# SSD scan: sample states on row quarters of TensorE, the D x term on VectorE, a held mask piece and later transposes of y

## The chip, the cores and the metric

One core of a Trainium2 chip runs the whole step. The metric is the device time of one execution in microseconds; the profile is one execution taken by the hardware profiler. Engines are named as in the profile: PE is TensorE, PEld its weight loads, DVE VectorE, ACT ScalarE, POOL GpSimd, SP SyncE.

## What is computed

One step of a hybrid encoder: a Mamba-2 (SSD) mixer, a PEER mixer, attention with a window, and a second PEER mixer, over 256 frames of one new stream and 16 frames of each of 8 running streams (384 rows in three blocks of 128; the third block holds the 8 samples, 16 rows each). The change lies in the SSD mixer, which in the reference comes to this:

```python
xbc, conv_new = causal_conv(xbc, conv_prev, conv_w, conv_b)      # 4 taps, then silu
dt = softplus(dt_raw + dt_bias); A = -exp(a_log)
acum = cumsum(dt * A)                                            # inside a chunk of 64 frames
lmat = exp(where(causal, acum_i - acum_j, -inf))
y_diag = einsum('bcijgr,bcjgrp->bcigrp', cb[..., None] * lmat, x * dt)      # cb = C B^T
states = einsum('bcjgn,bcjgrp->bcgrpn', B, x * dt * exp(acum_end - acum))
s_fin, s_prev = scan(s * chunk_decay + states)
y = y_diag + einsum('bcign,bcgrpn->bcigrp', C, s_prev) * exp(acum)
y = rmsnorm((y + x * d_skip) * silu(z)) @ w_out
```

There are 32 heads of 64 channels in 8 groups, a state of 128 for each, and for the 8 running streams an old state per head that is decayed, updated and written out.

## The kernel before

The scan runs over the eight groups, `for g in range(GROUPS)`. For each group four convolution tiles are made: `b_tile`, `c_tile`, `x_tile(0)`, `x_tile(1)`. One is a gemm of 24 matmuls of 128x384 (L130 to L132, high and low halves of an fp32 split) into one PSUM bank, copies by ScalarE, a first tap by ScalarE (L368), three taps by VectorE (L371), and a silu by ScalarE (L373, L374). The split of each block of weights is a cast by ScalarE (L105, `hi`) and a subtraction by VectorE (L106, `lo`). `gate` is the gemm for z (L425 to L427).

`decay` builds the masked decay matrix `ab`: twelve VectorE pieces (L438), one exponential by ScalarE (L441, before which it loads a table, as it does again for the next silu), the product C B^T on TensorE (L444) and one VectorE product (L446); it also transposes B (L449) and copies it (L451) and, with ScalarE, makes eight copies of the sample block of B, each masked to one sample (L453). `tokens` transposes x (L461) and scales it (L463). A group later, `states` makes the prompt's states (L471 to L475); `outputs` sums per head the D x term (a diagonal `dg`, made by POOL at L397, times `xs`, L483) and the masked product (L487) in PSUM, makes the old-state term (L490, and L494 on column quarters of the array), and VectorE puts y together (L499 to L503). `turn` transposes y (L512) and splits it (L108, L109) for w_out. `carry` decays the samples' old states (L518), computes the eight samples' new states as eight matmuls over all 128 rows with the masked copies (L523) into four banks, and adds them (L525).

After the eight groups the product with w_out runs over 16 blocks of channels (`out_terms`); the last group's states and outputs come at block 2, its turn at 5, its carry at 7. Six PSUM banks are its accumulators; there are eight in all.

A scheduler sets the order of each engine's instructions from its own estimate of times; each engine runs its list strictly in that order. `pin` is the one means by which the program forces a place: the instruction stays behind the one that the program wrote just before it for the same engine.

## Time and profile before

| | us |
|---|---|
| median of 3 runs | 2582.8 |
| lowest and highest | 2578.8, 2591.1 |
| the profiled execution | 2576.94 |
| its span | 2575.2 |
| PE busy in the span | 2425.7 |
| DVE busy | 1927.6 |
| ACT busy | 1313.5 |
| POOL busy | 683.2 |

The share of busy time is a mean over stages with different limits. The scan and w_out fill the first 400 us, the first peer layer follows, then attention and the second peer layer. A stage is read by its own stretch, and an order by the timeline. A row that has no bracket at its end followed the row before it on its engine without a wait.

### The profile page before, as it was taken

The numbers are of one execution on the slowest core, as the hardware profiler recorded it, in microseconds if no ns is written. First come the engines' busy times: TensorE is split into PE (matmuls) and PEld (weight loads), VectorE is DVE, ScalarE is ACT, GpSimd is POOL, SyncE is SP. The second block draws the span as 40 slices with busy tenths as digits, with TensorE's granted clock in tenths as the row PEclk, the third lists the DMA queues.
The fourth block names the chain that finished last, engine by engine and source line by source line (L and its number), as shares of the span: only waits on it lengthen the run. The fifth ranks groups of instructions, "written<-read, shape, count | busy, mean of one in ns | idle before, by whom it ended". The sixth has DMA issues, their size and how long they took to land. (4 is left out here: it accounts for less than half of the span.)

```text
span 2575.2 us, 45047 instructions
## 1 busy us (share of the span) xinstructions
PE 2425.7 (94%) x16816; PEld 2055.6 (80%) x16816; DVE 1927.6 (75%) x4206; ACT 1313.5 (51%) x2522; POOL 683.2 (27%) x749
## 2 busy tenths in 40 slices
PE   8999999999899999999998998999899999999998
PEld 7999988988789976666666878998789976667666
DVE  5877746989989988765455656989989988765445
ACT  5756524433456666554444544443456665554444
POOL 2222200033332244432331100033332244433331
PEclk9999999999999999999999989999999999999999
DMA  5545434478888899988886314478788898888886
GB/s 183 181 168 178 147 128 148 146 263 276 266 297 285 296 323 334 350 306 307 318 319 208 125 42 157 140 270 274 263 294 286 294 333 330 339 302 305 302 315 231
DMA packets 179117, 645.62 MB, mean 251 GB/s; under 512 B 24193, under 2 KB 26097, under 8 KB 176241
## 3 DMA queue, kind: packets, MB, share of 16 engines
q1 hardware_dynamic: 99632, 366.90, 40.6%
q0 software_dynamic: 79264, 275.84, 31.1%
q8 instruction: 132, 2.16, 0.3%
q14 instruction: 89, 0.72, 0.1%
HBM read 626.43 MB, written 18.06 MB: 250 GB/s over the span
## 5 line engine op out<-in xcount | busy, mean ns | idle before, releaser
L105 ACT CAST hi<-raw 128x1024 fp32r<-128x1024 f32 (+1 forms) x616 | 641.5, 1042 | 650.5 <-PE bank L131 425.7
L106 DVE TENSOR_TENSOR lo<-raw,hi 128x1024 fp32r<-128x1024 f32 (+1 forms) x616 | 750.0, 1218 | 234.3 <-ACT hi L105 233.2
L1072 POOL DMA_INDIRECT gath<-in_p_u,eidU x256 | 297.8, 1163 | 796.6 <-DVE gath L1109 424.0
L132 PE MATMUL bank<-xhi,lo 128*128 128x256 f32 (+1 forms) x1344 | 408.3, 304 | 12.6 <-DVE lo L106 12.5
L130 PE MATMUL bank<-xhi,hi 128*128 128x256 f32 (+1 forms) x1344 | 404.2, 301 | 4.2 <-ACT hi L105 4.2
L131 PE MATMUL bank<-xlo,hi 128*128 128x256 f32 (+1 forms) x1344 | 398.5, 297 | 0.0
L132 PE MATMUL bank<-qhi,lo 128*128 128x256 f32 (+1 forms) x1152 | 349.0, 305 | 29.7 <-DVE lo L106 29.5
L130 PE MATMUL bank<-qhi,hi 128*128 128x256 f32 (+1 forms) x1152 | 348.3, 303 | 19.6 <-ACT hi L105 12.0
L1109 DVE SCALAR_TENSOR_TENSOR gath<-gath,xg 128x1024 f32<-128x1024 f32 x256 | 311.8, 1218 | 50.2 <-DMA gath<-in_p_u,eidU 50.1
L131 PE MATMUL bank<-qlo,hi 128*128 128x256 f32 (+1 forms) x1152 | 344.3, 299 | 0.0
L143 PE MATMUL bank<-lo,phi 128*128 128x512 f32 x1024 | 331.6, 405 | 6.3 <-DVE lo L106 5.9
L143 PE MATMUL bank<-hi,plo 128*128 128x512 f32 x1024 | 322.7, 397 | 0.0
L143 PE MATMUL bank<-hi,phi 128*128 128x512 f32 x1024 | 291.6, 405 | 16.8 <-ACT hi L105 13.6
L105 ACT CAST phi<-G 128x256 fp32r<-128x256 f32 x256 | 103.4, 405 | 378.7 <-PE bank L143 264.9
L1072 POOL DMA_INDIRECT gv<-in_p_v,eidT x180 | 203.6, 1131 | 326.0 <-PE bank L1126 277.2
L132 PEld LDWEIGHTS bank<-xhi,lo 128*128 128x128 f32 x1344 | 255.4, 190 | 20.0 <-DVE lo L106 17.6
L143 PEld LDWEIGHTS bank<-hi,phi 128*128 128x128 f32 x1024 | 186.3, 189 | 96.4 <-ACT hi L105 41.0
L130 PEld LDWEIGHTS bank<-xhi,hi 128*128 128x128 f32 x1344 | 255.9, 190 | 8.8 <-ACT hi L105 5.2
L131 PEld LDWEIGHTS bank<-xlo,hi 128*128 128x128 f32 x1344 | 255.6, 190 | 0.3
L132 PEld LDWEIGHTS bank<-qhi,lo 128*128 128x128 f32 x1152 | 223.3, 195 | 36.5 <-DVE lo L106 36.2
L130 PEld LDWEIGHTS bank<-qhi,hi 128*128 128x128 f32 x1152 | 223.7, 194 | 23.5 <-ACT hi L105 15.1
L143 PEld LDWEIGHTS bank<-lo,phi 128*128 128x128 f32 x1024 | 187.2, 190 | 66.5 <-DVE lo L106 16.5
(343 smaller groups left out, 3889.1 us busy)
## 6 DMA issues: line engine op xcount, KB each, us to landing
raw<-in_u_t SPq DMA_DIRECT2D x256, 512.0 KB, 4.6
raw<-in_p_v SPq DMA_DIRECT2D x256, 512.0 KB, 5.5
raw<-in_w_in SPq DMA_DIRECT2D x32, 512.0 KB, 4.8
raw<-in_p_w_q SPq DMA_DIRECT2D x32, 512.0 KB, 5.5
s<-in_state_ssm SPq DMA_DIRECT2D x8, 1024.0 KB, 4.8
raw<-in_w_z SPq DMA_DIRECT2D x16, 512.0 KB, 3.8
out_sm_ssm<-s SPq DMA_DIRECT2D x8, 1024.0 KB, 4.2
raw<-in_w_out SPq DMA_DIRECT2D x16, 512.0 KB, 4.3
```

The source lines that it names most:

```text
L105: act.copy(hi, raw)
L106: dve.tensor_tensor(lo, raw, hi32, op=OP.subtract)
L130: pe.matmul(ps, whi[:, s], xhi[:, k, c0:c1], start=(k == 0), stop=False)
L131: pe.matmul(ps, whi[:, s], xlo[:, k, c0:c1], start=False, stop=False)
L132: pe.matmul(ps, wlo[:, s], xhi[:, k, c0:c1], start=False, stop=(k == KD - 1))
L143: mm = pe.matmul(ps, x, w[:, hf * n:(hf + 1) * n], start=s_, stop=e_)
L1072: pool.indirect_dma_start(out=tile_, out_offset=None, in_=tab, in_offset=bass.IndirectOffsetOnAxis(ap=idx, axis=0))
L1109: pin(dve.scalar_tensor_tensor(tile_, tile_, 1.0, xg[g], op0=OP.mult, op1=OP.mult, accum_out=au[g][:, j:j + 1]))
```

## The change

It does four things. The samples' states are made by eight matmuls that each read 32 of the 128 rows (two samples) with a mask that keeps one of the two, so `Bt` has two masked copies in place of eight; quarter q writes bank q, and both passes `w` go round the four banks; each is pinned. The D x term leaves TensorE: VectorE computes x times `dsk` into y where it scales x, the old-state term goes to a tile `yo` of its own, and y is summed from the three; the factor silu(z) is applied to the whole of y at the end. In `decay` the first of the twelve mask pieces is pinned behind the VectorE instruction written just before, which is the last tap of the convolution before it (of `x_tile(1)` of the same group, and for group 0 of `c_tile` of group 1); the decay of the old states is pinned behind `turn`. The transposes of y and the carry are called between `x_tile(0)` and `x_tile(1)`, and not before `x_tile(0)` (for group 0, after `x_tile(1)` of group 1).

```diff
@@ -253,8 +253,7 @@
-            dsk = T(one, [P, 16], F32, tag="dsk")
-            sync.dma_start(dsk, t_in["d_skip"])
+            dsk = brow(t_in["d_skip"], HEADS, one, "dsk")
 
...
+            parm = T(one, [P, 2], F32, tag="parm")
...
                     dve.tensor_scalar(seqm, iob[:, :NSEQ], seqf, None, op0=OP.is_equal)
+                    dve.tensor_reduce(parm, seqm.rearrange("p (q w) -> p w q", w=2), axis=AX.X, op=OP.add)
@@ -392,9 +394,6 @@
...
                         self.s0 = T(two, [P, NSEQ, 256], F32, tag="s0")
                         sync.dma_start(self.s0, t_in["state_ssm"][g])
-                        self.dg = T(two, [P, 2, P], F32, tag="dg", bufs=1)
-                        for j in range(2):
-                            pool.tensor_scalar(self.dg[:, j], ident, dsk[:, 2 * g + j:2 * g + j + 1], None, op0=OP.mult)
 
                     def b_tile(self):
                         self.BT = T(two, [P, NT], F32, tag="BT")
@@ -435,9 +434,9 @@
                         ab = self.ab
                         for rr in range(4):
                             for b in range(NB):
-                                dve.scalar_tensor_tensor(ab[:, rr, b], ab[:, rr, b],
+                                (pin if rr + b == 0 else lambda i_: i_)(dve.scalar_tensor_tensor(ab[:, rr, b], ab[:, rr, b],
                                                          acum[:, b, 4 * g + rr:4 * g + rr + 1], msk[:, b],
-                                                         op0=OP.subtract, op1=OP.add)
+                                                         op0=OP.subtract, op1=OP.add))
                         act.activation(ab, ab, AF.Exp)
                         cb = bank([P, NB, P])
                         for b in range(NB):
@@ -447,14 +446,15 @@
                         pb = bank([P, NB, P])
                         for b in range(NB):
                             pe.transpose(pb[:, b], BT[:, b * P:(b + 1) * P], ident)
-                        self.Bt = Bt = T(two, [P, 2 + NSEQ, P], F32, tag="Bt", bufs=1)
+                        self.Bt = Bt = T(two, [P, 4, P], F32, tag="Bt", bufs=1)
                         act.copy(Bt[:, 0:2], pb[:, 0:2])
-                        for i in range(NSEQ):
-                            act.activation(Bt[:, 2 + i], pb[:, 2], AF.Copy, scale=seqm[:, i:i + 1])
+                        for w in range(2):
+                            act.activation(Bt[:, 2 + w], pb[:, 2], AF.Copy, scale=parm[:, w:w + 1])
 
                     def tokens(self):
                         self.xdt = T(two, [P, NB, 256], F32, tag="xdt", bufs=1)
                         self.xde = T(two, [P, NB, 256], F32, tag="xde", bufs=1)
+                        self.y = T(two, [P, NB, 256], F32, tag="y", bufs=1)
                         for b in range(NB):
                             px = bank([P, 256])
                             for j in range(2):
@@ -462,6 +462,8 @@
                             for o, sc in ((self.xdt, dt), (self.xde, ddt)):
                                 dve.tensor_tensor(heads(o[:, b]), heads(px),
                                                   sc[:, b, self.hs].unsqueeze(2).to_broadcast([P, 4, 64]), op=OP.mult)
+                            dve.tensor_tensor(heads(self.y[:, b]), heads(px),
+                                              dsk[:, self.hs].unsqueeze(2).to_broadcast([P, 4, 64]), op=OP.mult)
 
                     def states(self):
 
@@ -479,13 +481,9 @@
                         pY = [bank([P, 256]), bank([P, 2, 256])]
                         for b in range(NB):
                             o = pY[0] if b == 0 else pY[1][:, b - 1]
-                            for j in range(2):
-                                pe.matmul(o[:, j * P:(j + 1) * P], self.xs[:, j, b * P:(b + 1) * P], self.dg[:, j],
-                                          start=True, stop=False)
-                                for rr in (2 * j, 2 * j + 1):
-                                    cs = slice(64 * rr, 64 * rr + 64)
-                                    pe.matmul(o[:, cs], self.ab[:, rr, b], self.xdt[:, b, cs], start=False,
-                                              stop=(rr == 2 * j + 1))
+                            for rr in range(4):
+                                cs = slice(64 * rr, 64 * rr + 64)
+                                pe.matmul(o[:, cs], self.ab[:, rr, b], self.xdt[:, b, cs], start=True, stop=True)
                         pO = bank([P, 2, 256])
                         pe.matmul(pO[:, 0], self.CT[:, P:2 * P], self.st[:, 0], start=True, stop=True)
                         for w in range(2):
@@ -494,13 +492,15 @@
                                 pe.matmul(pO[rows, 1], self.CM[:, w, q].rearrange("p w t -> p (w t)"),
                                           self.s0[:, 2 * q + w], start=(w == 0), stop=(w == 1),
                                           tile_position=(0, 32 * q))
-                        y = self.y = T(two, [P, NB, 256], F32, tag="y", bufs=1)
-                        y12 = y[:, 1:].rearrange("p b (r d) -> p b r d", d=64)
-                        dve.tensor_tensor(y12, pO.rearrange("p b (r d) -> p b r d", d=64),
+                        y = self.y
+                        yo = T(two, [P, 2, 256], F32, tag="yo", bufs=1)
+                        dve.tensor_tensor(yo.rearrange("p b (r d) -> p b r d", d=64),
+                                          pO.rearrange("p b (r d) -> p b r d", d=64),
                                           etok[:, :, self.hs].unsqueeze(3).to_broadcast([P, 2, 4, 64]), op=OP.mult)
-                        dve.tensor_tensor(y[:, 0], self.zs[:, 0], pY[0], op=OP.mult)
+                        dve.tensor_tensor(y[:, 1:], y[:, 1:], yo, op=OP.add)
+                        dve.tensor_tensor(y[:, 0], y[:, 0], pY[0], op=OP.add)
                         dve.tensor_tensor(y[:, 1:], y[:, 1:], pY[1], op=OP.add)
-                        dve.tensor_tensor(y[:, 1:], y[:, 1:], self.zs[:, 1:], op=OP.mult)
+                        dve.tensor_tensor(y, y, self.zs, op=OP.mult)
                         for b in range(NB):
                             act.activation(self.zs[:, b], y[:, b], AF.Square, accum_out=ssq[:, b, g:g + 1])
 
@@ -515,12 +515,16 @@
                     def carry(self):
 
                         s0 = self.s0
-                        dve.tensor_tensor(s0.rearrange("p s (r d) -> p s r d", d=64),
-                                          s0.rearrange("p s (r d) -> p s r d", d=64),
-                                          decS[:, :, self.hs].unsqueeze(3).to_broadcast([P, NSEQ, 4, 64]), op=OP.mult)
+                        pin(dve.tensor_tensor(s0.rearrange("p s (r d) -> p s r d", d=64),
+                                              s0.rearrange("p s (r d) -> p s r d", d=64),
+                                              decS[:, :, self.hs].unsqueeze(3).to_broadcast([P, NSEQ, 4, 64]),
+                                              op=OP.mult))
                         pss = [bank([P, 2, 256]) for _ in range(4)]
-                        for i in range(NSEQ):
-                            pe.matmul(pss[i // 2][:, i % 2], self.Bt[:, 2 + i], self.xde[:, 2], start=True, stop=True)
+                        for w in range(2):
+                            for q in range(4):
+                                rows = slice(32 * q, 32 * q + 32)
+                                pin(pe.matmul(pss[q][:, w], self.Bt[rows, 2 + w], self.xde[rows, 2],
+                                              start=True, stop=True, tile_position=(32 * q, 0)))
                         for k in range(4):
                             dve.tensor_tensor(s0[:, 2 * k:2 * k + 2], s0[:, 2 * k:2 * k + 2], pss[k], op=OP.add)
 
@@ -548,16 +552,17 @@
                     if g == 0:
                         st_ = steps()
                         next(st_)
-                    if g > 1:
-                        prev.turn()
                     G_.x_tile(0)
                     if g == 1:
                         prev.states()
                         prev.outputs()
+                    elif g:
                         prev.turn()
-                    if g:
                         prev.carry()
                     G_.x_tile(1)
+                    if g == 1:
+                        prev.turn()
+                        prev.carry()
                     if g == 0:
                         G_.gate()
                         next(st_, None)
@@ -1323,7 +1328,7 @@
     a["conv_b"] = f["m_conv_b"][0].reshape(32, P).T
     a["dt_bias"] = f["m_dt_bias"][0]
     a["a_log"] = f["m_a_log"][0]
-    a["d_skip"] = np.repeat(f["m_d_skip"][0], 64).reshape(16, P).T
+    a["d_skip"] = f["m_d_skip"][0]
     a["m_norm"] = f["m_norm"][0].reshape(16, P).T
     a["w_out"] = f["m_w_out"][0]
     a["state_conv"] = f["state_conv"][0].reshape(NSEQ, 3, 32, P).transpose(3, 2, 0, 1)
```

What this does to the order on the engines at three places:

TensorE in a steady group, before: states (L471), outputs (L483 to L494), and further down the samples' states (L523) with the transposes of y (L512).

```order
L471 MATMUL bank_1945<-xde_1875,Bt_1771 128x256
L483 MATMUL bank_1951<-dg_1533,xs_1641 128x128
L471 MATMUL bank_1945<-xde_1875,Bt_1771 128x256
L487 MATMUL bank_1951<-xdt_1874,ab_1529 128x64 x2
L483 MATMUL bank_1951<-dg_1533,xs_1641 128x128
L487 MATMUL bank_1951<-xdt_1874,ab_1529 128x64 x2
L483 MATMUL bank_1952<-dg_1533,xs_1641 128x128
L487 MATMUL bank_1952<-xdt_1874,ab_1529 128x64 x2
```

```order
L523 MATMUL bank_2096<-xde_1875,Bt_1771 128x256 x2
L523 MATMUL bank_2097<-xde_1875,Bt_1771 128x256 x2
L523 MATMUL bank_2098<-xde_1875,Bt_1771 128x256 x2
L523 MATMUL bank_2099<-xde_1875,Bt_1771 128x256 x2
L512 MATMUL bank_2037<-ident_69,y_1981 128x128 x2
L512 MATMUL bank_2043<-ident_69,y_1981 128x128 x2
```

The same places after the change (line numbers differ: L473 is L471, L486 is L487, L488 is L490, L492 is L494, L526 is L523):

```order
L473 MATMUL bank_2307<-xde_2236,Bt_2138 128x256
L486 MATMUL bank_2313<-xdt_2235,ab_1904 128x64 x3
L473 MATMUL bank_2307<-xde_2236,Bt_2138 128x256
L486 MATMUL bank_2313<-xdt_2235,ab_1904 128x64
L486 MATMUL bank_2314<-xdt_2235,ab_1904 128x64 x8
L488 MATMUL bank_2327<-st_2306,CT_1948 128x256
L492 MATMUL bank_2327<-s_314_1906,cm_55_247 32x256 x8
```

```order
L512 MATMUL bank_2440<-ident_69,y_2237 128x128 x3
L512 MATMUL bank_2446<-ident_69,y_2237 128x128 x3
L526 MATMUL bank_2453<-xde_2236,Bt_2138 128x256
L526 MATMUL bank_2454<-xde_2236,Bt_2138 128x256
L526 MATMUL bank_2455<-xde_2236,Bt_2138 128x256
L526 MATMUL bank_2456<-xde_2236,Bt_2138 128x256
L526 MATMUL bank_2453<-xde_2236,Bt_2138 128x256
L526 MATMUL bank_2454<-xde_2236,Bt_2138 128x256
L526 MATMUL bank_2455<-xde_2236,Bt_2138 128x256
L526 MATMUL bank_2456<-xde_2236,Bt_2138 128x256
```

The matmuls with `dg` are gone from the outputs, the transposes of y stand ahead of the samples' states, and these go round four banks twice.

VectorE in the first group, before: `ab_609` is the decay matrix of group 0, `ab_759` that of group 1, `cv_672` the convolution of b of group 1, `cv_718` that of c.

```order
L438 SCALAR_TENSOR_TENSOR ab_609<-ab_609,acum_238,msk_245 128x128 x12
L438 SCALAR_TENSOR_TENSOR ab_759<-ab_759,acum_238,msk_245 128x128 x4
L106 TENSOR_TENSOR lo_771<-raw_768,hi_770 128x1024
L438 SCALAR_TENSOR_TENSOR ab_759<-ab_759,acum_238,msk_245 128x128 x8
L371 SCALAR_TENSOR_TENSOR cv_672<-xp_665,convw_218,cv_672 128x408
L446 TENSOR_TENSOR ab_609<-ab_609,bank_740 128x1536
L106 TENSOR_TENSOR lo_890<-raw_887,hi_889 128x1024
L371 SCALAR_TENSOR_TENSOR cv_672<-xp_665,convw_218,cv_672 128x408
```

After, `ab_611` is the matrix of group 0, `ab_756` that of group 1, and `cv_675`, `cv_721`, `cv_799` are the convolutions of b, c and x of group 1:

```order
L373 SCALAR_TENSOR_TENSOR cv_721<-xp_714,convw_218,cv_721 128x408
L373 SCALAR_TENSOR_TENSOR cv_675<-xp_668,convw_218,cv_675 128x408
L106 TENSOR_TENSOR lo_952<-raw_949,hi_951 128x1024
L475 TENSOR_TENSOR st_806<-st_806,dec_47_239 128x256
L373 SCALAR_TENSOR_TENSOR cv_721<-xp_714,convw_218,cv_721 128x408
L477 TENSOR_TENSOR st_806<-st_806,bank_807 128x256
L373 SCALAR_TENSOR_TENSOR cv_799<-xp_792,convw_218,cv_799 128x408
L373 SCALAR_TENSOR_TENSOR cv_721<-xp_714,convw_218,cv_721 128x408
L437 SCALAR_TENSOR_TENSOR ab_611<-ab_611,acum_238,msk_246 128x128
L373 SCALAR_TENSOR_TENSOR cv_799<-xp_792,convw_218,cv_799 128x408 x2
L445 TENSOR_TENSOR ab_611<-ab_611,bank_743 128x1536
L501 TENSOR_TENSOR y_617<-y_617,bank_813 128x256
```

Of the twelve pieces for group 0 eleven stay ahead of these rows, in one run; the pinned one and the product behind it moved behind the convolutions of b and c.

TensorE at the end of w_out. Before, the last samples' states (L523) stand among the products with blocks far from the last (the end of w_out is some 165 rows further on):

```order
L523 MATMUL bank_3756<-xde_3507,Bt_3403 128x256
L143 MATMUL bank_3523<-hi_3773,yhi_234 128x512
L523 MATMUL bank_3757<-xde_3507,Bt_3403 128x256 x2
L143 MATMUL bank_3524<-hi_3773,yhi_234 128x512
L143 MATMUL bank_3523<-lo_3774,yhi_234 128x512
L143 MATMUL bank_3524<-lo_3774,yhi_234 128x512
```

After, six of the eight stand at the last products of w_out, right ahead of the peer layer's transposes (L892, which is L887 before):

```order
L143 MATMUL bank_3455<-lo_3873,yhi_234 128x512
L526 MATMUL bank_3679<-xde_3430,Bt_3332 128x256
L143 MATMUL bank_3454<-hi_3872,ylo_233 128x512
L526 MATMUL bank_3680<-xde_3430,Bt_3332 128x256
L526 MATMUL bank_3677<-xde_3430,Bt_3332 128x256
L526 MATMUL bank_3678<-xde_3430,Bt_3332 128x256
L526 MATMUL bank_3679<-xde_3430,Bt_3332 128x256
L526 MATMUL bank_3680<-xde_3430,Bt_3332 128x256
L143 MATMUL bank_3455<-hi_3872,ylo_233 128x512
L892 MATMUL bank_3989<-ident_69,qTp_3947 128x128
```

They moved from the middle of w_out to its last three products.

## Rows read from the trace of the kernel before

**Rows 1.** Busy time in stretches, three groups of the scan from one L444 to the next. Columns: stretch, its length, busy us and (instructions) of PE, PEld, DVE, ACT, POOL, the granted clock, DMA share, GB/s.

```profile
123.45:160.99 37.54, 37.54 (x264) 36.02 (x264) 30.86 (x54) 23.02 (x50) 10.08 (x21) 1.00 0.49 177
160.99:198.53 37.54, 37.54 (x264) 36.02 (x264) 29.70 (x51) 23.02 (x50) 10.29 (x20) 1.00 0.46 165
198.53:236.06 37.53, 37.53 (x264) 36.02 (x264) 29.69 (x51) 23.01 (x50) 10.29 (x20) 1.00 0.47 166
```

**Rows 2.** Timeline of TensorE (PE) in one group, 174 to 199 us. Columns here and in every timeline: start us, us until the last of the row ends, engine, line, operation, out<-in, count, and in brackets the idle time before and its releaser. A fp32 matmul is two instructions.

```profile
175.35 0.59 PE L471 MATMUL bank<-xde,Bt 128*128 128x256 f32 x2
175.78 0.38 PE L483 MATMUL bank<-dg,xs 128*128 128x128 f32 x2
...
176.82 0.44 PE L483 MATMUL bank<-dg,xs 128*128 128x128 f32 x2
177.10 0.56 PE L487 MATMUL bank<-xdt,ab 128*128 128x64 f32 x4
...
180.17 0.65 PE L490 MATMUL bank<-st,CT 128*128 128x256 f32 x2
180.75 1.07 PE L494 MATMUL bank<-s,cm 128*32 128x256 f32 x16
...
190.48 3.62 PE L523 MATMUL bank<-xde,Bt 128*128 128x256 f32 x16
193.93 0.60 PE L512 MATMUL bank<-ident,y 128*128 128x128 f32 x4
```

**Rows 3.** Timeline of TensorE in the attention stage, 1446 to 1450 us: the scores of 64-row halves.

```profile
1447.00 1.14 PE L727 MATMUL bank<-kT,qT 64*128 64x256 f32 x8
```

**Rows 4.** Groups of VectorE's instructions by line and shape, 145 to 370 us. Columns: line, engine, operation, names and shapes, count, busy us, mean ns of one, idle before and its releasers.

```profile
L525 DVE TENSOR_TENSOR s<-s,bank 128x512 f32<-128x512 f32 x24 | 16.3, 684 | 12.5 <-PE bank L523 12.5
...
L438 DVE SCALAR_TENSOR_TENSOR ab<-ab,acum,msk 128x128 f32<-128x128 f32 x48 | 13.0, 348 | 0.0
L446 DVE TENSOR_TENSOR ab<-ab,bank 128x1536 f32<-128x1536 f32 x5 | 8.8, 1755 | 3.2 <-PE bank L444 3.2
...
L463 DVE TENSOR_TENSOR xdt<-bank,dt 128x256 f32<-128x256 f32 x15 | 6.3, 419 | 12.0 <-PE bank L461 12.0
...
L503 DVE TENSOR_TENSOR y<-y,zs 128x512 f32<-128x512 f32 x6 | 4.1, 690 | 0.1
L502 DVE TENSOR_TENSOR y<-y,bank 128x512 f32<-128x512 f32 x6 | 4.1, 681 | 0.0
```

**Rows 5.** Timeline of ScalarE (ACT) in a group, 160 to 199 us.

```profile
163.16 1.69 ACT L453 ACTIVATE Bt<-bank,seqm 128x128 f32<-128x128 f32 x6
...
188.38 1.28 ACT L441 ACT_TABLE_LOAD   x1
189.68 1.49 ACT L441 ACTIVATE ab<-ab 128x1536 f32<-128x1536 f32 x1
```

**Rows 6.** Timeline of VectorE (DVE) in the first group, 56 to 97 us.

```profile
60.64 4.29 DVE L438 SCALAR_TENSOR_TENSOR ab<-ab,acum,msk 128x128 f32<-128x128 f32 x16 [6.61 <-DMA ab<-acum_rows]
64.85 1.22 DVE L106 TENSOR_TENSOR lo<-raw,hi 128x1024 fp32r<-128x1024 f32 x1
...
68.63 1.75 DVE L446 TENSOR_TENSOR ab<-ab,bank 128x1536 f32<-128x1536 f32 x1
```

**Rows 7.** Timeline of ScalarE in the same stretch.

```profile
63.91 1.48 ACT L441 ACTIVATE ab<-ab 128x1536 f32<-128x1536 f32 x1 [3.64 <-DVE ab L438]
...
72.34 1.28 ACT L373 ACT_TABLE_LOAD   x1
73.63 0.42 ACT L373 ACTIVATE BT<-cv 128x256 f32<-128x256 f32 x1
```

**Rows 8.** Timeline of TensorE in the same stretch.

```profile
66.12 0.44 PE L132 MATMUL bank<-xhi,lo 128*128 128x384 f32 x1 [2.56 <-DVE lo L106]
66.40 0.34 PE L130 MATMUL bank<-xhi,hi 128*128 128x384 f32 x1
66.58 0.34 PE L131 MATMUL bank<-xlo,hi 128*128 128x384 f32 x1
...
70.97 0.61 PE L483 MATMUL bank<-dg,xs 128*128 128x128 f32 x4
```

**Rows 9.** Busy time in stretches at the beginning of the first peer layer; columns as in rows 1.

```profile
408.00:411.00 3.00, 2.38 (x7) 2.38 (x8) 3.00 (x6) 3.00 (x9) 0.00 (x0) 0.50 0.48 173
411.00:414.00 3.00, 3.00 (x12) 3.00 (x12) 0.45 (x1) 0.13 (x1) 0.00 (x0) 0.59 0.06 12
414.00:417.00 3.00, 3.00 (x19) 3.00 (x18) 0.00 (x0) 0.78 (x1) 0.00 (x0) 1.00 0.13 45
```

**Rows 10.** Timeline of TensorE there, 394 to 412 us: the first matmuls of the peer layer's query.

```profile
408.62 0.69 PE L130 MATMUL bank<-qhi,hi 128*128 128x384 f32 x1 [3.63 <-ACT xf L889]
409.11 0.52 PE L131 MATMUL bank<-qlo,hi 128*128 128x384 f32 x1
409.43 0.52 PE L132 MATMUL bank<-qhi,lo 128*128 128x384 f32 x1
```

**Rows 11.** Timeline of VectorE there, 396 to 409 us.

```profile
399.83 1.41 DVE L600 SCALAR_TENSOR_TENSOR h<-bank,rs,h 128x512 f32<-128x512 f32 x2 [0.25 <-PE bank L143]
...
403.09 0.75 DVE L876 TENSOR_SCALAR qTp<-h,rstd 128x1024 f32<-128x1024 f32 x1 [0.65 <-POOL rstd L168]
```

## The prediction

> **What bounds the kernel now.** I read the busy time in stretches first. The edits lie in the scan of the eight head groups, the first sixth of the span. Three stretches of one group each show TensorE busy for all of 37.5 us, at the full clock, while VectorE is busy 29.7 to 30.9 us and ScalarE 23.0 us [rows 1]. So a steady group is bound by TensorE; VectorE has some 7.8 us to spare and ScalarE 14.5. What the change takes from TensorE there comes off the time until VectorE, or a chain through it, is late. Then I read TensorE's timeline within a group [rows 2], VectorE's groups of instructions [rows 4], ScalarE's [rows 5], and the two places where the order is not the steady one: the first group [rows 6 to 8] and the passage from w_out into the first peer layer [rows 9 to 11]. The rest, some 2,170 us, isn't edited; its orders differ only by small reshuffles in the two stretches where the peer layers read their v table.
>
> **TensorE in a steady group: the D x term.** L483 goes. A pair of its instructions stands from 176.82 to 177.10, the start of the next, so 0.28 us; six pairs with the first at about 0.22 make 1.6 us [rows 2]. I take 1.5, since L487 (now L486) stays as it is but for its own start of the accumulation.
>
> **TensorE: the sample states.** L523 is 16 instructions from 190.48 to the start of L512 at 193.93: 3.45 us, 216 ns each [rows 2]. The new L526 has as many instructions and as many columns, but each uses 32 rows of the array, and four that follow each other use four different quarters and four different banks. No trace of before shows row quarters. Two rows are near. L494 packs by column quarters: 16 instructions of the same 256 columns from 180.75, 1.07 us in all, four at a time [rows 2]. In the attention stage L727 takes 64-row halves: 8 instructions with their weight loads in 1.14 us, where eight one by one at 216 ns would be 1.73; the figure holds the end of the last one too, so the halves do run beside each other [rows 3]. Bounds: 1.0 us (as L494) and 3.45 us (no overlap). I take 1.0, since L727 shows that row tiles overlap, on the same fp32 type. That is 2.45 us less.
>
> The row of L490 speaks against it: its pair takes 0.58 us (180.17 to 180.75) before the quarters of L494 begin, where L471's pair takes 0.43 (175.35 to 175.78): 0.15 us for a change of tiling [rows 2]. L526 adds two such changes a group, 0.3 us. The Trainium skill, "TensorEngine Tiling (Array Packing)", section Key Properties, says that a change of tiling mode makes TensorE drain; the 0.15 us agrees. The Trainium skill, "TensorE: Matmul & The Clock Gate", Part 3, gives a measured 3.07 for four row tiles: an estimate from it, 3.45 / 3.07 = 1.12 us, would take 0.1 us a group from the gain.
>
> So TensorE's own sum falls by 1.5 + 2.45 - 0.3 = 3.65 us, from 37.5 to 33.9.
>
> **VectorE in a steady group.** It gains three L465 of 128x256, each as an L463 of 419 ns; back to back such instructions start some 85 ns closer than they last (16 of L438, 348 ns each, take 4.21 us from 60.64 to 64.85, 263 ns apart [rows 4, 6]), so 3 x 0.33 = 1.0 us. L500 is a further 128x512 add, as L502: 0.6 us. L503 grows from 512 to 768 columns: by the difference of L502 (681 ns) and L463, 0.26 us [rows 4]. Sum +1.9, so 31.6 us busy of 33.9. That is a load which TensorE's time still covers, but only by 2.3 us. The hold adds a chain: the pinned one of the twelve mask pieces (L438, now L437), done last, is queued behind the last piece of x_tile(1)'s convolution; only then can ScalarE load its table (1.28 us) and take the exponential (1.49 us) [rows 5], and VectorE multiply by cb (1.76 us) [rows 4]; what is queued behind this on VectorE is the split of the next weights, and on TensorE the outputs. With the orders laid against each other, that product ends about 35 us into a cycle whose outputs come at 39: 3.7 us to spare. The outputs' D term no longer passes through TensorE; y is ready some 4 us before its transposes, which now stand one convolution later, in front of L526. ScalarE loses six of eight masked copies (L453, 1.69 us for six) [rows 5], off the path. POOL loses its two dg; it bounds nothing.
>
> I take 3.5 us a group, 0.15 of it lost to small waits now that VectorE stands at 31.6 of 33.9, 93%. Six groups (those in which the carries of groups 1 to 6 fall): **-21.0 us**. Bounds: 9 (no overlap of quarters) to 23.5 (1.5 + 2.45 six times, no switches).
>
> **The first group.** Here the hold has another meaning. In the kernel before, VectorE did all 12 pieces of group 0 (and four of group 1) in one run from 60.64, as soon as their rows had landed; exp at 63.91; the product L446 at 68.63; so TensorE went through L471 and L483 at 70.97 without a wait [rows 6 to 8]. In the changed order eleven pieces stand there, and the twelfth comes behind the convolutions of both b and c and the first piece of x_tile(0). That piece of x_tile(0) needs ScalarE's copies of x_tile(0), which come after TensorE's gemm and, on ScalarE, behind the state copy, a table load (72.34, 1.28 us) and the silu of b (73.63) [rows 7]. Followed through: state copy to 70.6, table 71.9, b's silu 72.5, copies 73.0, cv 73.8, VectorE's three pieces 75.2; ScalarE's silu of c, table load 76.9, exp 78.4, product with cb about 79.5 to 80. TensorE has L473 done at about 69.5, and its next instructions, L486, need that product: a gap of **10 us** that was not there. On the other side the split lo comes one run of pieces (1.3 us) earlier, which shortens the 2.56 us wait of L132 [rows 8]. L486 starts at 79.5 where L483 started at 70.97: 8.5 us late. From there the group has 1.5 + 2.4 us less to do, but y is late for its transposes by about 1.9, and TensorE runs its next matmuls at the half clock: after the 3.63 us gap at 408.62 the granted clock was 0.50, then 0.59, and full from 414 on; a matmul of 384 columns was spaced 0.32 us (409.11 to 409.43) instead of 0.18 (66.40 to 66.58), some 15 of them, so about 2.2 us lost [rows 8 to 10]. I take 2.4, as the outputs' small matmuls come first. Together 8.5 - 3.9 + 1.9 + 2.4 = **+8.9 us**. Bounds: -3 (the pieces and exp slide in front after all; the group then gains as the others) and +12 (no gain from L526).
>
> **w_out and the passage to peer.** The last outputs and the last carry save 3.7 us of TensorE as elsewhere. But the carry now needs four banks, each for both of its passes, while six accumulators hold six of eight; five of its quarters, four L529 (0.6 us each, as L525 [rows 4]) and the last transposed blocks come to stand at the very end of w_out. There VectorE is on the path: h at 399.83, qTp at 403.09, and TensorE restarts at 408.62 [rows 10, 11]. 2.4 us of L529 go in between, of which some 0.7 fall into waits. 3.7 - 1.7 = **-2 us**; bounds -4 and +1.
>
> **Sum.** -21.0 + 8.9 - 2.0 = -14.1 us. The profiled execution took 2576.94 us with a span of 2575.2; that makes 2562.8. The median of three is 2582.8, 5.9 above the profiled one; on it the forecast is **2568.7 us**, -0.55%. The v stretches are reordered by the scheduler with no work added: 0 +- 4 us.
>
> **Rivals.** *A. The quarters don't overlap*: L526 at 216 ns each. For it: no row shows row quarters; against it: L727. Then six groups give 9, the first group +11.4, w_out about 0: +2.4, 2585 us. *B. VectorE, or the chain by exp, becomes the bound*: 31.6 busy plus the 1.28 + 1.49 us in which it may have nothing else to do is 34.4, with a split late behind it 35.7. Gain 1.8 a group, 10.8: total -3.9, 2579 us. For it: 93% busy in strict order; against it: the layout has other pieces to fill. *C. Slower: the hold makes TensorE wait in every group*, as in the first. Place: L486 behind the product L445. It decides from the point where that product is more than 3.7 us later than I laid it out; 5 us beyond that point the period is 33.8 + 5 = 38.8, and six groups lose 7.8: 7.8 + 8.9 - 2 = +14.7, 2598 us. Against it: in a steady group the whole gate and the next b gemm stand on TensorE between that product and its use. *D. The first group doesn't stall*: -21 - 3 - 2 = -26, 2557 us. For it: half of the 10 us hangs on ScalarE's order at one place; against it: that order is the one the program has.
>
> **How the numbers follow.** 0.5% of the median, 12.9 us, is about what a measurement of this kernel can tell from no change: the border of faster is 2569.9. Forecast 0.57 with its own range 2560 to 2578, which straddles that border: 0.33 faster, 0.24 within. A 0.08, within. B 0.13, within. C 0.08, slower. D 0.14, faster. So faster 0.47, same 0.45, slower 0.08. The range reaches from D with the noise of the v stretches, 2553, to A, 2586, and leaves out C and the tails.
>
> **What would show it.** Period of the steady groups by starts of L443: 33.9 to 34.2 (36.4 under A, 35.7 under B, over 38 under C). L526: 16 instructions in about 1.0 us, starts in fours. A gap on TensorE before the first L486 of about 10 us with VectorE's product as releaser, and a clock at the half level behind it (none under D). VectorE busy 93% of a steady group. The start of the first peer gemm 14 us earlier. If the periods fall as said and the total doesn't, the loss lies in the v stretches.

## The result

The change makes the kernel slower: 2599.5 us against 2581.7 us (medians of eight runs each), ratio 1.0077 with a 95% interval of 1.0054 to 1.0099. The forecast was 2568.7 us, its range 2553 to 2586. The profiled execution has a span of 2590.4 us, 15.2 more than before.

Where it went is read from four marks on TensorE: the product C B^T (L444, now L443) of groups 0, 1 and 7, and the first matmul of the peer layer. Before the change the fourth is in [rows 10] at 408.62, and the first three are:

```profile
62.05 0.83 PE L444 MATMUL bank<-CT,BT 128*128 128x128 f32 x6
...
84.41 0.83 PE L444 MATMUL bank<-CT,BT 128*128 128x128 f32 x6
...
311.15 0.83 PE L444 MATMUL bank<-CT,BT 128*128 128x128 f32 x6
```

The same four marks after the change:

```profile
58.54 0.83 PE L443 MATMUL bank<-CT,BT 128*128 128x128 f32 x6
...
94.51 0.94 PE L443 MATMUL bank<-CT,BT 128*128 128x128 f32 x6
...
316.24 0.83 PE L443 MATMUL bank<-CT,BT 128*128 128x128 f32 x6
...
419.54 0.69 PE L130 MATMUL bank<-qhi,hi 128*128 128x384 f32 x1 [2.92 <-ACT xf L894]
```

| stretch, us | before | after | measured | forecast |
|---|---|---|---|---|
| first group, mark 1 to 2 | 22.36 | 35.97 | +13.6 | +8.9 |
| six groups, mark 2 to 3 | 226.74 | 221.73 | -5.0 | -21.0 |
| w_out and passage, mark 3 to 4 | 97.47 | 103.30 | +5.8 | -2.0 |

That is +14.4 in place of -14.1. Ahead of mark 1 the changed kernel was 3.5 us earlier, and behind mark 4 it was 4.3 us longer. The change edits nothing behind mark 4; from there to the end the traces of this study lie between 2152 and 2180 us whatever the kernel, so this part is left alone.

**The steady groups.** Busy time in two of them, columns as in rows 1:

```profile
243.66:279.97 36.31, 34.79 (x252) 32.70 (x252) 31.08 (x55) 21.04 (x44) 9.64 (x18) 1.00 0.49 170
279.97:316.24 36.27, 34.53 (x253) 32.70 (x253) 31.50 (x47) 21.05 (x44) 8.66 (x18) 1.00 0.49 164
```

The period is 36.3 us, 1.2 less than in rows 1, and TensorE is now idle for 1.5 to 1.7 us of it. The first three of the six are longer, 37.5, 38.7 and 36.7 us. Over all six, TensorE stood idle for 12.8 us in place of 0.5, and its busy time fell by 17.3 us where 3.65 a group would make 21.9. What it waits for, over the first 425 us (columns: what waited and for what, us in total, times, longest):

```profile
PE bank L486 <- DVE ab L445: 10.2, 1, 10.2
PE bank L424 <- DVE s L529: 9.9, 6, 1.8
...
PE bank L892 <- DVE qTp L881: 6.7, 1, 6.7
...
PE bank L512 <- DVE y L503: 2.6, 2, 1.4
```

The waits of L424 and L892 are not in the forecast. TensorE in one group (columns as in rows 2):

```profile
246.94 0.39 PE L424 MATMUL bank<-hi,xhi 128*128 128x256 f32 x1 [1.52 <-DVE s L529]
...
260.00 0.59 PE L473 MATMUL bank<-xde,Bt 128*128 128x256 f32 x2
260.43 0.78 PE L486 MATMUL bank<-xdt,ab 128*128 128x64 f32 x6
261.04 0.65 PE L473 MATMUL bank<-xde,Bt 128*128 128x256 f32 x2
261.53 2.12 PE L486 MATMUL bank<-xdt,ab 128*128 128x64 f32 x18
263.48 0.65 PE L488 MATMUL bank<-st,CT 128*128 128x256 f32 x2
264.06 1.07 PE L492 MATMUL bank<-s,cm 128*32 128x256 f32 x16
...
273.62 0.82 PE L512 MATMUL bank<-ident,y 128*128 128x128 f32 x6
274.37 1.15 PE L526 MATMUL bank<-xde,Bt 32*128 32x256 f32 x16
```

By these rows the edits themselves came out near their price. L526 takes 1.07 us to the start of the next gemm, against 3.45 for L523; states and outputs from 260.00 to 264.06 take 4.06 us, against 5.40 in [rows 2] (175.35 to 180.75), so the D x term is worth 1.34. But the gate's third block of rows waits 1.52 us for L529. VectorE in the same group:

```profile
242.40 1.14 DVE L109 SCALAR_TENSOR_TENSOR ylo<-bank,ng,yhi 128x384 fp32r<-128x384 f32 x2
243.45 2.28 DVE L518 TENSOR_TENSOR s<-s,decS 128x2048 f32<-128x2048 f32 x1
...
246.20 2.47 DVE L529 TENSOR_TENSOR s<-s,bank 128x512 f32<-128x512 f32 x4
...
256.32 1.75 DVE L445 TENSOR_TENSOR ab<-ab,bank 128x1536 f32<-128x1536 f32 x1 [2.09 <-ACT ab L440]
...
270.96 0.88 DVE L437 SCALAR_TENSOR_TENSOR ab<-ab,acum,msk 128x128 f32<-128x128 f32 x3 [2.93 <-DMA ab<-acum_rows]
271.76 0.95 DVE L503 TENSOR_TENSOR y<-y,zs 128x768 f32<-128x768 f32 x1
```

L529, which frees the four banks of the sample states, stands behind the decay L518 (2.28 us), and L518 is pinned behind the split of the turned y at 242.40. By the releaser, a bank that L529 still has to read isn't free for the gate, so TensorE stops until the first of the four L529 is done, at 246.88, and goes on at 246.94. Two idle times of VectorE stand there too: 2.09 us for the exponential behind the held piece, and 2.93 us for the rows of the next group's matrix, whose pieces (L437) stand ahead of y's last step L503 in spite of the hold.

In the kernel before, the decay was not pinned. VectorE, then the gate's first matmul on TensorE:

```profile
182.50 2.28 DVE L518 TENSOR_TENSOR s<-s,decS 128x2048 f32<-128x2048 f32 x1
...
188.44 0.69 DVE L503 TENSOR_TENSOR y<-y,zs 128x512 f32<-128x512 f32 x1
...
196.14 0.69 DVE L525 TENSOR_TENSOR s<-s,bank 128x512 f32<-128x512 f32 x1
```

```profile
199.44 0.37 PE L425 MATMUL bank<-hi,xhi 128*128 128x256 f32 x1
```

There the last of the four adds (L525, now L529) was done at 196.83, 2.6 us ahead of the gate.

**The first group.** TensorE, VectorE and the busy time of the stretch:

```profile
77.81 5.35 PE L486 MATMUL bank<-xdt,ab 128*128 128x64 f32 x24 [10.20 <-DVE ab L445]
82.96 1.17 PE L488 MATMUL bank<-st,CT 128*128 128x256 f32 x2
84.06 1.94 PE L492 MATMUL bank<-s,cm 128*32 128x256 f32 x16
...
92.66 0.85 PE L512 MATMUL bank<-ident,y 128*128 128x128 f32 x6 [1.19 <-DVE y L503]
```

```profile
72.36 0.34 DVE L437 SCALAR_TENSOR_TENSOR ab<-ab,acum,msk 128x128 f32<-128x128 f32 x1
...
75.91 1.75 DVE L445 TENSOR_TENSOR ab<-ab,bank 128x1536 f32<-128x1536 f32 x1 [1.92 <-ACT ab L440]
```

```profile
66.00:90.00 24.00, 13.80 (x68) 11.46 (x67) 13.38 (x25) 9.75 (x15) 3.00 (x10) 0.64 0.25 83
```

The held piece runs at 72.36, its product at 75.91, and TensorE stands for 10.20 us. Then the granted clock: 0.64 in the mean of 66 to 90 us, so for the most part at the half level. The 24 L486 take 5.15 us (to 82.96), where the steady group takes 2.56 (0.61 + 1.95).

**The end of w_out.** VectorE, then TensorE:

```profile
405.03 1.87 DVE L529 TENSOR_TENSOR s<-s,bank 128x512 f32<-128x512 f32 x3
...
410.92 2.08 DVE L881 TENSOR_SCALAR qTp<-h,rstd 128x1024 f32<-128x1024 f32 x3 [2.16 <-DMA out_sm_ssm<-s]
```

```profile
403.52 1.13 PE L526 MATMUL bank<-xde,Bt 32*128 32x256 f32 x10
...
411.77 4.85 PE L892 MATMUL bank<-ident,qTp 128*128 128x128 f32 x24 [6.70 <-DVE qTp L881]
```

Ten of the sixteen instructions of the last carry stand at 403.52, ahead of the last matmul of w_out. L529 follows, then the store of the states, issued at 406.93, and L881, which makes the first blocks for the peer layer, waits for that store until 410.92 (its releaser is DMA out_sm_ssm). TensorE stands for 6.70 us, where in the trace before its longest wait at this place was 0.74.

### The profile page after: what moved, and what is told of

Same layout as the page of the kernel before. It is cut to its first block, busy times and chain, and to the rows that moved or that the text cites. A ratio compares the mean times of both kernels' runs of the same rounds, so it can differ in the third digit from the quotient of the medians.

```text
span 2590.4 us, 44838 instructions
## 1 busy us (share of the span) xinstructions
PE 2410.1 (93%) x16718; PEld 2031.3 (78%) x16720; DVE 1940.4 (75%) x4239; ACT 1303.0 (50%) x2478; POOL 677.6 (26%) x733
## 3 DMA queue, kind: packets, MB, share of 16 engines
q8 instruction: 131, 2.15, 0.3%
## 5 line engine op out<-in xcount | busy, mean ns | idle before, releaser
L132 PE MATMUL bank<-xhi,lo 128*128 128x256 f32 (+1 forms) x1344 | 407.9, 304 | 11.2 <-DVE lo L106 11.0
L132 PE MATMUL bank<-qhi,lo 128*128 128x256 f32 (+1 forms) x1152 | 348.5, 304 | 26.9 <-DVE lo L106 26.7
L143 PE MATMUL bank<-hi,phi 128*128 128x512 f32 x1024 | 296.2, 408 | 19.8 <-ACT hi L105 14.1
L132 PEld LDWEIGHTS bank<-xhi,lo 128*128 128x128 f32 x1344 | 254.0, 189 | 19.8 <-DVE lo L106 16.7
L132 PEld LDWEIGHTS bank<-qhi,lo 128*128 128x128 f32 x1152 | 222.8, 194 | 33.7 <-DVE lo L106 33.1
```

Source lines behind the costliest of these rows:

```text
L132: pe.matmul(ps, wlo[:, s], xhi[:, k, c0:c1], start=False, stop=(k == KD - 1))
L143: mm = pe.matmul(ps, x, w[:, hf * n:(hf + 1) * n], start=s_, stop=e_)
```

## The experiments

Ratios are against the kernel before, measured beside each run. Marks as above; a period is the time from one L443 to the next.

**1. First group free.**

```diff
-(pin if rr + b == 0 else lambda i_: i_)(...)
+(pin if rr + b == 0 and g else lambda i_: i_)(...)
```

> The changed kernel with the mask piece of group 0 free again; the pieces of groups 1 to 7 stay held. Theory: the gap of 10.20 us on TensorE before the first L486 comes from this one piece, and the half clock behind it with it. Then the gap is under 1 us, the start of L443 of group 1 lies 22 to 24 us behind that of group 0 (35.97 in the changed kernel, 22.36 in the one before), and the time is 11 to 14 us under the changed kernel. Rival: the first group is late because of the doubled calls behind x_tile(1) and the work that VectorE has more of; then the two L443 stay more than 30 us apart and the time changes by under 4 us.

Ratio 1.0051 (1.0030 to 1.0073). The 10.20 us are gone, mark 1 to 4 falls from 361.0 to 348.5 us, 12.5 less. So the held piece of group 0 is the cause of that stall. But mark 1 to 2 is 27.92 us, not 22 to 24: the transposes now wait 5.32 us for y, and the clock of 66 to 90 us is 0.85, better than 0.64 but not full. The ratio shows less than the marks: it fell by 0.0026, some 7 us, and its interval overlaps that of the changed kernel. The gate's waits for L529 fell too, from 9.9 to 6.6 us in six groups.

**2. Decay free.**

```diff
-pin(dve.tensor_tensor(s0..., decS..., op=OP.mult))
+dve.tensor_tensor(s0..., decS..., op=OP.mult)
```

> The changed kernel with the decay of the old states (L518) not pinned; it then stands in front of y's sum on VectorE again. Theory: the first matmul of the gate waits 1.4 to 1.8 us a group for L529, since L518 is held behind the split of the turned y and L529 queues behind L518 while it holds the banks that the gate needs. Without the pin this wait is under 0.4 us a group and the steady period falls from 36.3 to 34.6 to 35.0 us; 6 to 9 us less in all. Rival: the carry is called one convolution later, so L529 comes too late for the gate whatever stands ahead of it; then the wait stays over 1 us a group. A second rival: y now comes 2.2 us later and the transposes L512 wait in place of the gate, period unchanged at 36 us.

Ratio 1.0103 (1.0081 to 1.0126). No wait for L529 is left, so the pinned decay made it. But the second rival is what happened, and more: the six periods are 34.1 to 40.7 us.

```profile
PE bank L512 <- DVE y L503: 18.4, 6, 4.4
```

```profile
238.64 2.28 DVE L518 TENSOR_TENSOR s<-s,decS 128x2048 f32<-128x2048 f32 x1
240.84 0.68 DVE L500 TENSOR_TENSOR y<-y,yo 128x512 f32<-128x512 f32 x1
243.08 2.98 DVE L437 SCALAR_TENSOR_TENSOR ab<-ab,acum,msk 128x128 f32<-128x128 f32 x11 [1.56 <-DMA ab<-acum_rows]
245.98 0.68 DVE L502 TENSOR_TENSOR y<-y,bank 128x512 f32<-128x512 f32 x1
...
248.27 0.95 DVE L503 TENSOR_TENSOR y<-y,zs 128x768 f32<-128x768 f32 x1
```

Free, the decay, and the pieces of the next group with their wait for rows, slide between the steps of y (L500, L502, L503), and six groups wait 2.0 to 4.4 us for it. They stood there in the kernel before too (L518 at 182.50, y's last step at 188.44), without a wait: there four of the six transposes stood behind the samples' matmuls, at 193.93 [rows 2].

**3. Last carry by bank.**

```diff
-for w in range(2):
-    for q in range(4):
+for w, q in ([(w, q) for w in range(2) for q in range(4)] if self.g < GROUPS - 1
+             else [(w, q) for q in range(4) for w in range(2)]):
```

> The changed kernel with the last group's eight sample-state matmuls in the order of banks (both passes of a bank, then the next), the other groups as they are. Theory: the round over four banks can't get two more banks while six accumulators are open, so it ends with w_out; L529 and the store of the states follow, and the first block for the peer layer, which is written where the states lay, waits for the store: the gap of 6.70 us on TensorE before L892. By bank the carry finishes in the middle of w_out, the gap is under 1.5 us, and the time falls by 5 to 7 us. Rival: the wait comes from VectorE's later h and norms, and stays over 4 us.

Mark 3 to 4 falls from 103.30 to 98.16 us, as expected, and the longest wait of L892 is 0.8 us.

The ratio, 1.0082 (1.0056 to 1.0108), doesn't show it: the rest of the program took 2179.9 us from mark 4 in this trace, the most of all.

**4. The three together**, the edits of runs 1 to 3.

> The changed kernel with all three undone: piece of group 0 free, L518 free, last group by bank. If the three causes add, it is 22 to 29 us under the changed kernel, about 2572, and 6 to 12 us faster than the kernel before. Rival: the causes hide one another (the bank wait goes, a wait of the transposes for y takes its place), and it lies within 5 us of the kernel before.

Ratio 1.0022 (0.9996 to 1.0048). The rival: six waits for y, 2.1 to 7.0 us, take the place of the others, and the first five periods are 36.9 to 40.0 us.

**5. No hold in any group.**

```diff
-(pin if rr + b == 0 else lambda i_: i_)(...)
+(lambda i_: i_)(...)
```

> The changed kernel with no mask piece held in any group. Tells what the hold is worth in the groups from 1 on, where it doesn't stall. Theory: without it the exponential with its two table loads slides ahead of c's silu, TensorE waits 2 to 3 us a group for it, and the steady period is 37.5 us or more. Rival: the hold costs and gives nothing there; period 36 to 36.5 us.

One run, 2590.9 us, too little for a ratio; the trace is read for its periods. The steady ones are 36.4 to 36.6 us: nearer to the rival. The wait for c's silu is there (0.5 us a group, 1.5 in the first), with one of 1.2 for a split; together they are as long as the wait for L529 that they replace. In the steady groups the hold gives as much as it takes.

**6. Row quarters alone**, on the kernel before, with the last group by bank as in run 3.

```diff
-for i in range(NSEQ):
-    act.activation(Bt[:, 2 + i], pb[:, 2], AF.Copy, scale=seqm[:, i:i + 1])
+for w in range(2):
+    act.activation(Bt[:, 2 + w], pb[:, 2], AF.Copy, scale=parm[:, w:w + 1])
...
-pe.matmul(pss[i // 2][:, i % 2], self.Bt[:, 2 + i], self.xde[:, 2], start=True, stop=True)
+pin(pe.matmul(pss[q][:, w], self.Bt[rows, 2 + w], self.xde[rows, 2],
+              start=True, stop=True, tile_position=(32 * q, 0)))
```

> The kernel before with the sample states on row quarters alone (two masked copies, the last group by bank); the D x term stays on TensorE and nothing is held on VectorE. Theory: the 16 instructions take 1.07 us in place of 3.45, nothing becomes late, the steady period falls from 37.54 to 35.2 to 35.5 us and the time by 13 to 18 us. Rival: a part of it is lost again in a wait for L529 or y, period over 36.2 us.

Ratio 0.9959 (0.9941 to 0.9978). One period of the six, and the matmuls:

```profile
197.02:232.32 35.30, 35.17 (x264) 33.27 (x264) 29.75 (x51) 21.22 (x45) 10.83 (x21) 1.00 0.50 174
```

```profile
226.59 1.15 PE L527 MATMUL bank<-xde,Bt 32*128 32x256 f32 x16
227.67 0.66 PE L514 MATMUL bank<-ident,y 128*128 128x128 f32 x4
```

35.3 us, 2.24 less, with VectorE as busy as before, and no wait; all six lie between 35.0 and 35.4. Only the first group has a new one, 7.55 us for y, since the pinned matmuls stand behind all transposes. It costs much of the gain: the six periods are 15.2 us shorter in sum, mark 1 to 2 is 10.9 us longer. By the ratio the time fell by some 10.5 us, less than the 13 to 18 expected.

**7. D x term alone**, on the kernel before, with the change's edits of `tokens` and `outputs`:

```diff
+dve.tensor_tensor(heads(self.y[:, b]), heads(px), dsk..., op=OP.mult)
...
-pe.matmul(o[:, j * P:(j + 1) * P], self.xs[:, j, b * P:(b + 1) * P], self.dg[:, j], start=True, stop=False)
...
+dve.tensor_tensor(y[:, 1:], y[:, 1:], yo, op=OP.add)
```

> The kernel before with the D x term on VectorE alone; the sample states stay on all rows, nothing is held. Theory: TensorE loses L483, 1.3 us a group, and VectorE has room; period 36.1 to 36.4 us, 8 to 11 us less. Rival: y comes later by the added steps and its transposes wait, period unchanged at 37.5 us.

Ratio 1.0202 (1.0164 to 1.0239): neither expectation. The first five periods are 44.5 to 46.7 us.

```profile
PE bank L509 <- DVE y L500: 47.6, 7, 11.4
```

```profile
218.49 1.51 PE L509 MATMUL bank<-ident,y 128*128 128x128 f32 x6 [6.61 <-DVE y L500]
```

As in run 2, decay and pieces stand between the steps of y (L497, L499 and L500 here). But by the times VectorE's load is the smaller part. Counted from the start of its period, y's last step ends 30.5 us in, against 28.1 in the kernel before; TensorE, however, comes to all six transposes 24.0 us in, ahead of the samples' matmuls. In the kernel before, four of the six come 32.9 us in, and only the two of the first block, which is ready early, come at 25.0. One product with silu(z) over the whole of y takes that early block away. Alone the D x term so costs some 7 us a group, part of it by a granted clock of 0.89 to 0.92 in the three groups from 141.19 to 277.51. The changed kernel, with the later transposes and the pinned decay, bears it, and run 5 shows that it does so without the hold; how much the later place gives and how much the pin was not tried apart.

**8. Decay and all twelve pieces behind y.** The decay is called right after y's last product, pinned; from group 2 on the pieces follow, each pinned; groups 0 and 1 free; last group by bank.

```diff
 dve.tensor_tensor(y, y, self.zs, op=OP.mult)
+pin(dve.tensor_tensor(s0..., decS..., op=OP.mult))
...
 prev.outputs()
+G_.pieces()
...
-(pin if rr + b == 0 else lambda i_: i_)(dve.scalar_tensor_tensor(ab[:, rr, b], ...))
+if g < 2:
+    self.pieces()
```

> The changed kernel with the last group by bank, the decay of the old states (L518 of the changed kernel) pinned right behind y's last product, all twelve mask pieces of the next group pinned behind that (from group 2 on), and no hold on the pieces of groups 0 and 1. Theory: y is late where work of the next group (mask pieces that wait for their rows, the decay) floats ahead of its last two steps, and the gate waits where the decay stands too far behind; with y, decay, pieces in this order neither TensorE's wait for y nor the one for L529 is over 0.5 us a group, and the steady period is 33.7 to 34.6 us. 8 to 14 us faster than the kernel before. Rival: VectorE is full; some split (L106) behind the twelve pieces comes late, the period stays at 36 us or more.

Ratio 0.9993 (0.9968 to 1.0018). Neither y nor L529 is waited for by a steady group, but the periods are 37.1 to 39.5 us: the product C B^T waits 2.2 to 2.7 us for c's silu. I took the exponential and its table loads, which stood ahead of that silu on ScalarE, for the cause. With the calls of transposes and carry as before:

> The same, with the transposes of y and the carry called where the kernel before calls them (transposes ahead of x_tile(0), carry behind it). Tells whether the later place is needed. Theory: with y early, its place costs or gives under 0.5 us a group. Rival: the transposes then wait for y by 2 us or more a group, period over 36 us.

Ratio 1.0022 (0.9999 to 1.0045), periods 36.6 to 38.7, the same wait; the later place is worth no clear amount here.

**9. Run 8 with the exponential held** from group 2 on, and the first matmul of each carry not pinned.

```diff
-act.activation(ab, ab, AF.Exp)
+(pin if g > 1 else lambda i_: i_)(act.activation(ab, ab, AF.Exp))
```

> The run with y, decay, mask pieces in this order, but with the exponential (from group 2 on) pinned on ScalarE behind the silu of x_tile(1), and the first of the sample-state matmuls not pinned. There TensorE waited 2.2 to 2.7 us a group for c's silu, which stood behind the exponential and two table loads. Theory: this wait goes, no other comes, the steady period is 33.9 to 34.8 us, and the time 9 to 15 us under the kernel before. Rival: the D x term's load on VectorE shows as another wait (a split, xs, or the product behind the exponential), and the period stays over 35.3 us, that of the row quarters alone.

Ratio 1.0008 (0.9987 to 1.0030), periods 36.6 to 38.3. My reading fell: the wait for c's silu is still 2.2 us. VectorE and ScalarE there:

```profile
255.41 2.29 DVE L512 TENSOR_TENSOR s<-s,decS 128x2048 f32<-128x2048 f32 x1
257.61 3.23 DVE L455 SCALAR_TENSOR_TENSOR ab<-ab,acum,msk 128x128 f32<-128x128 f32 x12
...
268.14 1.87 DVE L373 SCALAR_TENSOR_TENSOR cv<-xp,convw,cv 128x408 f32<-128x408 f32 x3
```

```profile
268.81 0.42 ACT L375 ACTIVATE CT<-cv 128x256 f32<-128x256 f32 x1 [4.96 <-DVE cv L373]
```

Decay and pieces keep VectorE from 255.41 to 260.76, other work without a pause to 268.14; the last tap of c's convolution is the first of the three there, and the silu waited 4.96 us for it. So it is VectorE's queue.

**10. Run 6 with the first matmul of each carry not pinned.**

```diff
-pin(pe.matmul(pss[q][:, w], ...))
+mm = pe.matmul(pss[q][:, w], ...)
+if w + q:
+    pin(mm)
```

> The kernel before with row quarters alone, as in the run before of that kind, but the first of a group's eight sample-state matmuls isn't pinned (the other seven stay behind it). There TensorE waited 7.55 us for y in the first group, since the pinned matmuls stood behind all of y's transposes. Theory: with the first one free they stand ahead of four of the six transposes as in the kernel before, the wait is under 1 us, the first two L446 (the product C B^T) lie 22 to 26 us apart in place of 33.3, and the time is 6 to 10 us lower: 0.990 to 0.994 of the kernel before. Rival: that wait was made up for elsewhere, and it stays at 0.996.

Ratio 0.9952 (0.9931 to 0.9973). Mark 1 to 2 is 23.2 us and the wait for y is gone; the next period is 38.6, so marks 1 to 4 take 337.3 us against 342.5 in run 6. This is the lowest ratio of the study; but 0.990 to 0.994 was expected, and the interval holds run 6's 0.9959, so the rival isn't ruled out.

**11. The change with the D x term back on TensorE**, first group free, last group by bank; the hold, the pinned decay and the later calls stay. The edit is that of run 7 backwards, with those of runs 1 and 3.

> The changed kernel with the D x term back on TensorE, the piece of group 0 free and the last group by bank; row quarters, the later call of transposes and carry, the held pieces of groups 1 to 7 and the pinned decay of the states stay. VectorE has 1.9 us a group less to do than in the changed kernel. Theory: the gate's wait for L529 comes from the pinned decay, not from VectorE's load, so it stays at 1.2 to 1.8 us a group, and the period is 36.4 to 37.2 us, against 35.3 with row quarters alone. Rival: VectorE's load makes L529 late; then the wait is under 0.5 us and the period 35.2 to 35.6 us.

Ratio 0.9966 (0.9951 to 0.9982). The wait for L529 (L533 here) is left in three of six groups:

```profile
PE bank L428 <- DVE s L533: 2.9, 3, 1.7
```

Neither theory alone. Run 1, which has the D x term on VectorE and the first group free as here, waits 6.6 us in six groups; without the 1.9 us of the D x term the pinned decay comes early enough in three of them. The pin makes the wait and VectorE's load makes it longer. Periods are 34.9 to 38.8 us; the longest holds a wait of 1.69 us and a clock of 0.96.

## Why the prediction was wrong

- **TensorE's terms held one by one, not in their sum.** Foretold 2.45 us for the row quarters less 0.3 for two changes of tiling, 2.15; run 6 measured 2.24 a group. Foretold 1.5 for the D x term, measured 1.34 in its rows. That row tiles overlap, taken from L727, was right. The Trainium skill, "TensorE: Matmul & The Clock Gate", Part 3, has a measured 3.07 for four row tiles of 512 columns. With 256 columns the trace shows 3.45 / 1.07 = 3.2, close to it. But in the six groups of the changed kernel TensorE's busy time fell by 17.3 us and not by 21.9; which rows lost the 4.6 us is open.
- **The step that failed is the layout of VectorE in a steady group.** I put 0.15 us a group for "small waits" at 93% load and priced one chain, through the exponential to the outputs. That chain did not make TensorE wait in a steady group. What I left out is that the change adds a second wait, the pinned decay, whose queue holds PSUM banks: L518, four L529, and behind them the gate. It cost 9.9 us in six groups, 1.5 to 1.7 in a steady one, of the 16.0 us by which they missed the forecast (21.0 less foretold, 5.0 measured); the busy time above is 4.6 more, and waits for y and a split are most of the rest. Run 2 shows that the pin makes this wait, run 11 beside run 1 that VectorE's 1.9 us lengthen it. (The outer bound of this stretch, 1.5 + 2.45 six times, is 23.7, not 23.5.)
- **Rival B named the direction.** It gave 35.7 us a period for a VectorE that is in the way; 36.3 was measured, with VectorE 31.1 to 31.5 us busy, close to the 31.6 foretold. In every order of the D x term on VectorE that was run (the change's, and runs 1 to 5 and 7 to 9) a wait stays: for L529, for y, for c's silu or a split. None of the ratios is clearly under 1. Rival C's 2598 us is close to the measured time by luck, not by its mechanism: L486 waits in the first group only.
- **The first group: the stall was right, what follows it was mis-sized.** Foretold a gap of 10 us from the held piece, measured 10.20; run 1 confirms the cause. L486 came 10.35 us later than L483 did, by mark 1, and not 8.5, as the wait of L132 stayed at 2.55 us. I took 2.4 us for the half clock; the outputs alone lost 4.0 (5.15 + 1.10 + 1.87 against 2.56 + 0.58 + 1.00). These two make 3.4 of the 4.7 us by which the stretch missed; the rest was not traced.
- **w_out: sign wrong.** I saw that the carry would end with w_out and priced its four L529 at 2.4 us. I missed that the store of the states follows them and that the peer layer's first tile waits for it. Run 3, which ends the carry earlier, shows the size, 5.1 us; that the tile lies where the states lay is inferred from the releaser, not tried apart.
- **The three waits hide one another** (run 4). With all three undone the ratio is 1.0022, and the six periods, 227.5 us in sum, are no shorter than in the kernel before. So adding up three repairs would have been wrong as well.

## What to carry to other kernels

Before moving work to an engine that is 80% busy, lay out its queue and ask of each instruction which PSUM bank or buffer it frees and who needs that next; a share of 93% says nothing of that. Ask too whether an edit joins steps that were ready at different times, as the one product over the whole of y did. A pin on one instruction of an in-order engine holds what is behind it too: here one decay held four banks, and one mask piece a whole group. Try the parts apart: the row quarters alone are worth 0.4 to 0.5%, and the rest of the change ate them.

## What was not expected of the hardware

A wait can cost more than its length. In run 8 a steady group with one wait of 2.7 us had a granted clock of 0.95 in the mean, and TensorE was busy 36.0 us for the same instructions that took 34.6 in the changed kernel, whose waits of 1.5 to 1.7 us left the clock at 1.00.

```profile
194.22:232.92 38.70, 36.01 (x252) 34.12 (x252) 32.26 (x56) 22.10 (x46) 7.08 (x19) 0.95 0.50 171
```

But in run 11 a group with a wait of 1.69 us had 0.96, and in run 9 five groups with one wait of 2.2 us each had 1.00 twice and 0.95 to 0.96 three times. So the length of the wait alone doesn't tell it; what does is open.
